# A hybrid decoder layer on one core: value products in wider columns, the solve's row spread in two fp32r passes, and a refitted order

## The chip, the core and the metric

One Trainium2 chip, one of its cores. The time is device microseconds of one execution of the whole kernel, as the median of several runs. The engines are called by their functions: TensorE multiplies matrices (PE in the profile, its weight loads PEld), VectorE (DVE), ScalarE (ACT) and GpSimd (POOL) work elementwise, and SyncE (SP) issues most transfers.

## The reference

One decoder layer on x of 512 tokens by 1024 channels, all in float32:

```
h = x @ w_in                                   # one combined projection
y_a = nsa_attention(...) @ w_nsa_out           # 8 heads, compressed + selected + sliding window, gated
y_b = gated_deltanet(...) @ w_gdn_out          # 4 heads, chunked, a triangular solve in each chunk
mix = (sigmoid(gate_a) * y_a + sigmoid(gate_b) * y_b) @ w_o
x = layer_norm(ALPHA * x + mix)
f = conv_ffn(x)                                # up, causal conv of width 3, silu gate, down
x = layer_norm(ALPHA * x + f)
```

In the attention, the selected and the window branch of a head each come to a causal softmax over 512 keys with a distance penalty, times values of 64 columns. With 8 blocks of 64 keys and the best 8 chosen, the selected branch sees all keys. In the DeltaNet part, each head has, for every chunk of 64 tokens, a unit lower triangular matrix `eye + m` whose inverse T is needed.

## The kernel before, in words

Float32 accuracy is kept by splitting an operand into a rounded high part and the remainder, both in the format fp32r, and multiplying in three passes: high by high, high by low, low by high. A plain fp32 product is also possible, and is used for small ones. Weights stream from memory in tiles; `split_w` (the lines L241 to L252) loads one, rounds the two halves to `wh` and subtracts to get `wl`. Which engine rounds and which subtracts is looked up in the table ENGINE under "wh" and "ws" with the tile's number.

The first stage, to about 345 us, holds both mixers. The work of the two is cut into named steps: i, j, v (key, query and value convolutions of a DeltaNet head), m, n, w (its matrix, the diagonal solve, the inverse), o, y (recurrence and gate), k, q, p, c (attention keys, queries, compressed branch), a and b (the first and the last three score units of an attention head), and g (merge gates). ORDER writes down their order, SHIFT moves each by a number of priority units, and a list scheduler orders each engine's instructions by the resulting priorities. ENGINE assigns single operations to VectorE, ScalarE or GpSimd. Projections for later steps run on TensorE between the small products of the mixers; their results lie in one of two accumulators of the name `gps`, until the convolution (`conv_silu`, L405 to L423) has read all its taps from it. A tap on VectorE reads the accumulator itself; for a tap on GpSimd, ScalarE reads it and GpSimd adds.

Value products. For each attention head there are six units of scores (`scores`), each of 128 queries, of one branch or of both. `flip` transposes the probabilities of one unit, and writes them as high and low (`pth`, L843, and `ptl`, L844) into slots of 128 columns, of which each branch has eight. The units come in the order: queries 256 to 383 and 384 to 511 of the first branch, the same of the second, then 0 to 127 and 128 to 255 of both together. After each second unit, the products with the values (L856) run over two slots at a time, 256 columns, into the accumulator `pout`; slot 6 holds zeros, for the key block that lies beyond the queries of its unit.

The solve. `gdn_tri` inverts the 16x16 diagonal blocks of a head. `lo` is the strictly lower part of m with its sign, `f16` its rows within blocks (L521), and the rows are spread over the partitions by a product with the constant `same` (L529), of a masked copy `gx` (L527), once for 512 columns and once for 256. Fifteen rounds of a multiply and an add on VectorE follow (L536, L537), then `z`. Tiles `lo`, `gx`, `m` and others share the three buffers of the tag "mid"; `m` lives on until the inverse has been built.

After the first stage come the output products of the mixers (lines L262 to L265 with `pm`, L1021 to L1023), the up-projection with its convolution (`pu`, L1100 to L1119), and the down-projection by a seven-product scheme of half matrices (L1147). For it GpSimd issues eight transfers of 2816 KB that add weight blocks in memory (`sums`, L281), during the up-projection.

Of the kernel before, what the change touches and what calls it, by code (L numbers as in the profile page):

```python
# [21 lines left out]
TT = 4  # L22
# [112 lines left out]
def body(ctx: ExitStack, tc: tile.TileContext, d, out):  # L135
    nc = tc.nc
    V, A, G, PE = nc.vector, nc.scalar, nc.gpsimd, nc.tensor

    def E(name, h, d="V"):

        return {"V": V, "G": G, "A": A}[ENGINE.get(f"{name}{h}", d)]

    def bc(ap, shape):
        return ap.to_broadcast(shape)
# [41 lines left out]
    nsa = Rows(ph1, "nsa", 1, side="right")  # L186
    sp = Rows(ph1, "slots", 1, side="right")
    def slot(tag, name, shape=(128, 512), dt=F32):
        return sp.tile(list(shape), dt, name=name, tag=tag, bufs=BUFS[tag])
# [324 lines left out]
    def gdn_tri(h):  # L514
        st = HS[h]
        m = st["m"]

        lo = slot("mid", "lo", c4)
        E("lo", h).tensor_tensor(lo, m, bc(C["low"][:, None, :], c4), op=OP.mult)
        f16 = sp.tile([128, TT, 16], F32, name="f16", bufs=2)  # L520
        V.tensor_reduce(f16, lo.rearrange("p c (b j) -> p c j b", b=8), axis=AX.X, op=OP.add)  # L521
        lx = slot("lx", "lx", (128, TT, 16, 16))
        for r0, n in ((8, 16), (0, 8)):
            rs = slice(r0, r0 + 8)
            sh = (128, TT, 8, n)
            gx = slot("mid", "gx", sh)
            E(f"gx{n}", h).tensor_tensor(gx, bc(f16[:, :, None, :n], sh), bc(C["row"][:, None, rs, None], sh), op=OP.mult)  # L527
            pl = dps(sh)
            PE.matmul(pl, C["same"], gx, start=True, stop=True)  # L529
            A.activation(lx[:, :, rs, :n], pl, AF.Copy)  # L530
        xs = sp.tile([128, TT, 16], F32, name="xs", bufs=2)
        E("xs", h).tensor_copy(xs, bc(C["row"][:, None, :], (128, TT, 16)))
        tmp = sp.tile([128, TT, 16], F32, name="tmp", bufs=2)
        for r in range(15):
            n = 15 - r
            V.tensor_tensor(tmp[:, :, :n], lx[:, :, r + 1:, r], bc(xs[:, :, r:r + 1], (128, TT, n)), op=OP.mult)  # L536
            V.tensor_tensor(xs[:, :, r + 1:], xs[:, :, r + 1:], tmp[:, :, :n], op=OP.add)  # L537
# [288 lines left out]
    def flip(h, u, s):  # L826
# [16 lines left out]
        A.activation(th, pt, AF.Copy)  # L843
        V.tensor_tensor(tl, pt, th.bitcast(F32), op=OP.subtract)  # L844
        if t % 2 == 0:
            return
        if u == 1:
            POUT[h] = po.tile([128, S], F32, name="pout")
        pout = POUT[h]
        for br, _ in parts:  # L850
            for k in range(4 if t > 1 else 2):
                o = pout[:, 256:] if t > 1 else pout[:, :256]
                b = 2 * k if t > 1 else 4 + 2 * k
                w = vcat[:, k, br, g].rearrange("p a b -> p (a b)")
                for i, src in enumerate((pth, ptl)):
                    PE.matmul(o, w, src[:, br, b:b + 2, :], start=(u == 1 and k == 0 and i == 0), stop=False)  # L856
# [409 lines left out]
```

## Time and profile before

| what | value |
|---|---|
| three runs | 851.35, 852.24 and 846.26 us, median 851.35 |
| profiled execution, its own time | 847.99 us |
| its span in the profile | 846.2 us |
| TensorE busy | 826.3 us, 98% |
| VectorE, ScalarE, GpSimd busy | 597.3, 403.0, 164.3 us |
| products of L856 | 192 |
| mean granted clock of TensorE | 0.992 |

Busy time is the share of the span in which an engine had at least one instruction under way. Matmuls overlap: one of 512 columns is shown with about 0.39 us while the next starts 0.23 us after it, so distances between starts give the cost. In rows of groups, the numbers behind the bar are the sum of busy time, the mean of one in ns, and the idle time of the engine before them with what ended it. In a timeline a row has its start, its length, the engine, the line and what is written from what.

### The profile page before, as it was taken

The numbers are of one execution on the slowest core, as the hardware profiler recorded it, in microseconds if no ns is written. First come the engines' busy times: TensorE is split into PE (matmuls) and PEld (weight loads), VectorE is DVE, ScalarE is ACT, GpSimd is POOL, SyncE is SP. The second block draws the span as 40 slices with busy tenths as digits, with TensorE's granted clock in tenths as the row PEclk, the third lists the DMA queues.
The fourth block names the chain that finished last, engine by engine and source line by source line (L and its number), as shares of the span: only waits on it lengthen the run. The fifth ranks groups of instructions, "written<-read, shape, count | busy, mean of one in ns | idle before, by whom it ended". The sixth has DMA issues, their size and how long they took to land.

```text
span 846.2 us, 11884 instructions
## 1 busy us (share of the span) xinstructions
PE 826.3 (98%) x4226; PEld 681.4 (81%) x4226; DVE 597.3 (71%) x1276; ACT 403.0 (48%) x890; POOL 164.3 (19%) x160
## 2 busy tenths in 40 slices
PE   9899899999999999999999999999999999999996
PEld 8777688777778778888888898888888888887874
DVE  5855579986867866674457637777777777768786
ACT  4464377575456777532234113444444444556531
POOL 0354442233136111102200003111112111100000
PEclk9999899999999999999999999999999999999998
DMA  7223111002101110254346007998975922575662
GB/s 273 95 83 100 54 48 51 26 26 75 45 32 66 35 51 26 88 178 134 125 137 237 25 2 269 266 244 253 205 223 153 225 88 77 161 247 176 198 213 100
DMA packets 35051, 108.05 MB, mean 128 GB/s; under 512 B 3248, under 2 KB 4400, under 8 KB 34608
## 3 DMA queue, kind: packets, MB, share of 16 engines
q1 hardware_dynamic: 27696, 84.23, 30.6%
q0 software_dynamic: 7296, 23.07, 11.5%
q8 instruction: 33, 0.54, 0.3%
q14 instruction: 26, 0.21, 0.1%
HBM read 105.19 MB, written 25.17 MB: 154 GB/s over the span
## 4 chain that ended last, share of the span: by engine, by line
PE 84%; DVE 10%; DMA 2%; issue 2%; ACT 1%; SPq 0%; POOL 0%; DVEq 0%; ACTq 0%; POOLq 0%
PE pu L262 9%; PE pu L264 9%; PE pu L265 9%; PE gps L262 7%; PE gps L264 7%; PE gps L265 7%; PE px L1147 5%; PE pz L1147 3%; PE pout L856 2%; PE aps L839 2%; PE pw L1022 2%; PE pw L1023 2%; PE pw L1021 2%; PE pm L265 2%; PE pm L262 2%; PE pm L264 2%
## 5 line engine op out<-in xcount | busy, mean ns | idle before, releaser
L252 DVE TENSOR_TENSOR wl<-raw,wh 128x512 fp32r<-128x512 f32 x140 | 114.1, 816 | 66.9 <-ACT wh L248 62.5
L248 ACT ACTIVATE wh<-raw 128x512 fp32r<-128x512 f32 x136 | 85.5, 631 | 151.4 <-PE pu L264 103.8
L262 PE MATMUL pu<-mh,wh 128*128 128x512 f32 (+1 forms) x384 | 142.7, 372 | 0.0
L264 PE MATMUL pu<-ml,wh 128*128 128x512 f32 (+1 forms) x384 | 142.6, 371 | 0.0
L265 PE MATMUL pu<-mh,wl 128*128 128x512 f32 (+1 forms) x384 | 142.6, 371 | 0.0
L262 PE MATMUL gps<-xh,wh 128*128 128x512 f32 x320 | 129.3, 405 | 3.6 <-DVE xs L537 2.2
L264 PE MATMUL gps<-xl,wh 128*128 128x512 f32 x320 | 129.1, 404 | 0.0
L265 PE MATMUL gps<-xh,wl 128*128 128x512 f32 x320 | 126.8, 398 | 0.0
L265 PEld LDWEIGHTS pu<-mh,wl 128*128 128x128 f32 x384 | 72.3, 188 | 12.6
L262 PEld LDWEIGHTS pu<-mh,wh 128*128 128x128 f32 x384 | 72.3, 188 | 12.4
L264 PEld LDWEIGHTS pu<-ml,wh 128*128 128x128 f32 x384 | 72.3, 188 | 12.4
L262 PEld LDWEIGHTS gps<-xh,wh 128*128 128x128 f32 x320 | 60.4, 189 | 16.6 <-issue 2.9
L1103 DVE SCALAR_TENSOR_TENSOR fa<-pu,fcw,fa 128x511 f32<-128x511 f32 x88 | 65.7, 746 | 10.7 <-ACT fa L1100 9.2
L265 PEld LDWEIGHTS gps<-xh,wl 128*128 128x128 f32 x320 | 60.6, 189 | 10.8 <-issue 0.2
L264 PEld LDWEIGHTS gps<-xl,wh 128*128 128x128 f32 x320 | 60.6, 189 | 10.2 <-issue 0.2
L1109 POOL TENSOR_TENSOR fth<-fth,fa 128x512 f32<-128x512 f32 x22 | 28.6, 1302 | 201.8 <-DVE fa L1103 201.8
L252 POOL TENSOR_TENSOR wl<-raw,wh 128x512 fp32r<-128x512 f32 x36 | 46.3, 1288 | 83.0 <-ACT wh L248 68.8
L1080 ACT ACTIVATE wh<-raw 128x512 fp32r<-128x512 f32 x67 | 40.5, 627 | 39.8 <-DMA raw<-wsum 11.1
L1081 DVE TENSOR_TENSOR wl<-raw,wh 128x512 fp32r<-128x512 f32 x67 | 43.8, 685 | 19.4 <-ACT wh L1080 19.2
L812 ACT ACTIVATE sc<-sc,mn 128x384 f32<-128x384 f32 (+2 forms) x64 | 35.8, 560 | 12.9 <-DVE mn L810 10.7
L295 POOL TENSOR_TENSOR rs<-rs,minus_half 128x1 f32<-128x1 f32 x8 | 7.6, 945 | 166.5 <-DVE rs L980 166.5
L1100 ACT ACTIVATE fa<-pu,fcw 128x512 f32<-128x512 f32 x44 | 29.6, 672 | 10.2 <-PE pu L265 10.2
(330 smaller groups left out, 1689.5 us busy)
## 6 DMA issues: line engine op xcount, KB each, us to landing
raw<-in_up SPq DMA_DIRECT2D x44, 512.0 KB, 4.8
raw<-in_wT SPq DMA_DIRECT2D x40, 512.0 KB, 3.5
wsum<-in_down POOLq DMA_DIRECT2D x6, 2816.0 KB, 24.5
raw<-wsum SPq DMA_DIRECT2D x20, 512.0 KB, 4.2
raw<-in_down SPq DMA_DIRECT2D x15, 512.0 KB, 4.4
wsum<-wsum POOLq DMA_DIRECT2D x2, 2816.0 KB, 12.3
raw<-in_wm SPq DMA_DIRECT2D x8, 512.0 KB, 3.6
raw<-in_wo SPq DMA_DIRECT2D x8, 512.0 KB, 3.6
```

The lines of the kernel that those rows point to most:

```text
L248: A.activation(wh, r, AF.Copy)
L252: eng.tensor_tensor(wl, r, wh.bitcast(F32), op=OP.subtract)
L262: i = PE.matmul(ps, wh[k], mh_(k), start=(k == 0), stop=False)
L264: PE.matmul(ps, wh[k], ml_(k), start=False, stop=False)
L265: PE.matmul(ps, wl[k], mh_(k), start=False, stop=(k == n - 1))
L812: A.activation(s[:, i, :n], s[:, i, :n], AF.Exp, scale=-1.0, bias=mn[:, 0, i:i + 1], accum_out=mn[:, 1, i:i + 1])
L1080: A.activation(hi, raw[:, i], AF.Copy)
L1081: V.tensor_tensor(lo, raw[:, i], hi.bitcast(F32), op=OP.subtract)
L1100: A.activation(acc, ps, AF.Copy, scale=w[:, 2:3])
L1103: V.scalar_tensor_tensor(acc[:, n:], ps[:, :S - n], w[:, i:i + 1], acc[:, n:], op0=OP.mult, op1=OP.add)
L1109: G.tensor_tensor(th, th, g[1], op=OP.mult)
L1147: m = PE.matmul(ps, a[x][:, j, ts], w[y], start=first and i == 0, stop=last and i == 2, skip_group_check=True)
```

## The change

Value products: the buffers for the probabilities get 13 slots a branch in place of 8, slot t + 3k for query block t and key block k. The units come in the order of the queries, the two short ones first. The products of a branch run when its last unit is there: key block 0 over all 512 query columns, block 1 over 384, blocks 2 and 3 over 256 each, with a zero slot for key block 3 of the third query block.

The solve: the constant `same` is copied to fp32r once, on GpSimd. `f16` gets three parts, of which the third is the sum as before, the first its rounding and the second the remainder. Each half of the row spread becomes two fp32r products into the same accumulator, of a masked copy of the high part and of one of the low.

Priorities: ORDER, SHIFT and ENGINE are replaced as a whole. The new ENGINE names an engine for nearly every choice, where many stood at a default before. Among others, it moves the last tap of head 1's query convolution ("cq10") from VectorE to GpSimd, `z`, `gx` and `gy` of head 0 in part to GpSimd, and a number of "ws" and "wh" between engines.

The space in on-chip memory that is set aside for the descriptors of GpSimd's transfers is set to 4096 bytes a partition.

```diff
-SHIFT = {'q0': -193, 'a0': -2348, ...
+SHIFT = {'q0': -145, 'a0': -3160, ...
-ENGINE = {'p16': 'A', 'p55': 'V', ...
+ENGINE = {'p36': 'V', 'p15': 'V', ...
-ORDER = "q0 k0 i0 q1 j0 m0 c n0 w0 i1 j1 v0 v1 p0 o0 a0 y0 b0 a1 b1 m1 a2 b2 n1 w1 i2 j2 o1 y1 m2 v2 a3 n2 q2 w2 b3 o2 y2 q3 g0 p1 k1 i3 j3 a4 b4 m3 a5 n3 w3 g1 g2 b5 v3 o3 a6 g3 b6 a7 g4 b7 g5 y3".split()
+ORDER = "q0 k0 i0 q1 j0 c m0 n0 w0 i1 j1 v0 p0 v1 o0 a0 y0 b0 a1 m1 b1 a2 n1 w1 b2 i2 j2 o1 y1 m2 n2 a3 v2 w2 q2 o2 q3 y2 g0 b3 k1 p1 i3 j3 m3 g1 a4 n3 b4 a5 g2 v3 w3 g3 b5 a6 b6 g4 a7 o3 b7 y3 g5".split()
...
+    same_r = nsa.tile([128, 128], F32R, name="same_r")
...
         V.tensor_copy(upper_r, C["upper"])
+        G.tensor_copy(same_r, C["same"])
...
-        f16 = sp.tile([128, TT, 16], F32, name="f16", bufs=2)
-        V.tensor_reduce(f16, lo.rearrange("p c (b j) -> p c j b", b=8), axis=AX.X, op=OP.add)
+        f16 = sp.tile([128, 3, TT, 16], F32, name="f16", bufs=2)
+        V.tensor_reduce(f16[:, 2], lo.rearrange("p c (b j) -> p c j b", b=8), axis=AX.X, op=OP.add)
+        V.tensor_copy(f16[:, 0].bitcast(F32R), f16[:, 2])
+        V.tensor_tensor(f16[:, 1], f16[:, 2], f16[:, 0], op=OP.subtract)
         lx = slot("lx", "lx", (128, TT, 16, 16))
         for r0, n in ((8, 16), (0, 8)):
             rs = slice(r0, r0 + 8)
             sh = (128, TT, 8, n)
-            gx = slot("mid", "gx", sh)
-            E(f"gx{n}", h).tensor_tensor(gx, bc(f16[:, :, None, :n], sh), bc(C["row"][:, None, rs, None], sh), op=OP.mult)
             pl = dps(sh)
-            PE.matmul(pl, C["same"], gx, start=True, stop=True)
+            for i, e in enumerate(("gx", "gy")):
+                gx = slot("mid", "gx", sh, F32R)
+                E(f"{e}{n}", h).tensor_tensor(gx, bc(f16[:, i, :, None, :n], sh), bc(C["row"][:, None, rs, None], sh),
+                                              op=OP.mult)
+                PE.matmul(pl, same_r, gx, start=(i == 0), stop=(i == 1))
             A.activation(lx[:, :, rs, :n], pl, AF.Copy)
...
-    pth = nsa.tile([128, 2, 8, 128], F32R, name="pth")
-    ptl = nsa.tile([128, 2, 8, 128], F32R, name="ptl")
+    pth = nsa.tile([128, 2, 13, 128], F32R, name="pth")
+    ptl = nsa.tile([128, 2, 13, 128], F32R, name="ptl")
     for t in (pth, ptl):
-        G.memset(t[:, :, 6, :].bitcast(F32), 0.0)
-    UNITS = [((0, 2),), ((0, 3),), ((1, 2),), ((1, 3),), ((0, 0), (1, 0)), ((0, 1), (1, 1))]
+        G.memset(t[:, :, 11, :].bitcast(F32), 0.0)
+    UNITS = [((0, 0), (1, 0)), ((0, 1), (1, 1)), ((0, 2),), ((0, 3),), ((1, 2),), ((1, 3),)]
...
-        first = t - 2 if t > 1 else 4 + t
-        own = (slice(br, br + len(parts)), slice(first, first + 2 * t + 1, 2))
+        own = (slice(br, br + len(parts)), slice(t, 4 * t + 1, 3))
...
-        if t % 2 == 0:
+        if t < 3:
             return
-        if u == 1:
+        if br == 0:
             POUT[h] = po.tile([128, S], F32, name="pout")
         pout = POUT[h]
-        for br, _ in parts:
-            for k in range(4 if t > 1 else 2):
-                o = pout[:, 256:] if t > 1 else pout[:, :256]
-                b = 2 * k if t > 1 else 4 + 2 * k
-                w = vcat[:, k, br, g].rearrange("p a b -> p (a b)")
-                for i, src in enumerate((pth, ptl)):
-                    PE.matmul(o, w, src[:, br, b:b + 2, :], start=(u == 1 and k == 0 and i == 0), stop=False)
-        if u < 5:
+        for k in range(4):
+            c = min(k, 2)
+            w = vcat[:, k, br, g].rearrange("p a b -> p (a b)")
+            for i, src in enumerate((pth, ptl)):
+                PE.matmul(pout[:, 128 * c:], w, src[:, br, 3 * k + c:3 * k + 4, :],
+                          start=(br == 0 and k == 0 and i == 0), stop=False)
+        if br == 0:
             return
...
-    nc = bacc.Bacc("TRN2", target_bir_lowering=False, num_devices=1)
+    nc = bacc.Bacc("TRN2", target_bir_lowering=False, num_devices=1, dynamic_dma_scratch_size=4096)
```

More of the change, by code (lines that the diff above doesn't have):

```diff
@@ L126 @@
 LATE = 2500
-SHIFT = {'q0': -193, 'a0': -2348, 'b0': -2285, 'a1': -2210, 'b1': -330, 'a2': -197, 'q3': -550, 'j3': -1663, 'a4': -1622, 'g2': 1524, 'o2': -2902, 'i1': -138, 'b5': -2781, 'y2': 147, 'q1': -7406, 'g1': -1529, 'y3': 6625, 'y1': 53, 'b3': -761, 'k0': -68, 'm2': -702, 'g3': 637, 'b6': 362, 'v2': 240, 'j1': -112, 'm0': -5504, 'b7': -5643, 'o3': 1155, 'y0': 203, 'q2': 4142, 'g4': -1463, 'm3': -2997, 'v0': -140, 'j0': -2134, 'v1': 41, 'o1': -4704, 'v3': 274, 'o0': -1428, 'n2': -847, 'g0': -122, 'b2': -55, 'k1': -1459, 'j2': 105, 'p0': 215, 'a3': 46, 'm1': -1324, 'n3': 240, 'n1': -1535, 'i0': -1541, 'a5': -49, 'p1': -115, 'i2': -71, 'i3': 77, 'n0': -13, 'a6': 272, 'g5': 1119, 'b4': -10, 'a7': 1035, 'w2': -801, 'w3': 118, 'w1': -1404, 'w0': 29, 'c': 6}
@@ L128 @@
-ENGINE = {'p16': 'A', 'p55': 'V', 'p24': 'A', 'p32': 'A', 'vb0': 'A', 'p43': 'A', 'p04': 'G', 'p54': 'A', 'p20': 'G', 'kd2': 'A', 'p25': 'A', 'kd0': 'V', 'p06': 'A', 'vb1': 'A', 'lo3': 'G', 'p44': 'A', 'p45': 'V', 'p34': 'G', 'p36': 'A', 'kd1': 'A', 'kd3': 'A', 'sq1': 'V', 'xs3': 'G', 'vb2': 'A', 'wh31': 'V', 'ws4': 'V', 'ws11': 'V', 'ws29': 'G', 'p03': 'V', 'wh2': 'A', 'wh43': 'G', 'p37': 'A', 'ws43': 'V', 'wh42': 'G', 'ws30': 'G', 'wh8': 'V', 'ws14': 'G', 'wh32': 'G', 'wh35': 'G', 'ws15': 'G', 'sq3': 'V', 'y1': 'V', 'z3': 'V', 'wh0': 'V', 'wh36': 'A', 'wh38': 'G', 'wh1': 'A', 'ws1': 'V', 'ws18': 'V', 'ws38': 'V', 'p26': 'V', 'wh39': 'G', 'sv2': 'V', 'sk0': 'G', 'p33': 'V', 'ws16': 'G', 'ws36': 'G', 'ws40': 'V', 'ws5': 'G', 'p47': 'V', 'xs2': 'G', 'ck2': 'V', 'wh34': 'A', 'ws21': 'G', 'wh46': 'G', 'ws42': 'V', 'wh47': 'G', 'ws32': 'V', 'wh44': 'V', 'ws34': 'V', 'ws39': 'V', 'lo0': 'G', 'gx80': 'V', 'gx81': 'G', 'gx82': 'G', 'gx83': 'V', 'xs1': 'G', 'ws27': 'G', 'sv0': 'G', 'ws0': 'V', 'wh5': 'A', 'wh22': 'A', 'ws9': 'V', 'wh6': 'A', 'wh17': 'A', 'cv1': 'V', 'wh37': 'G', 'ws25': 'V', 'ws17': 'V', 'ws20': 'V', 'wh14': 'V', 'wh30': 'A', 'cv2': 'G', 'wh33': 'V', 'ws28': 'V', 'cv21': 'G', 'ws35': 'G', 'wh24': 'V', 'ck0': 'G', 'y2': 'A', 'p46': 'A', 'ck1': 'G', 'ck30': 'V', 'p07': 'A', 'p56': 'A', 'y3': 'V', 'z2': 'G', 'ws13': 'G', 'ws12': 'V', 'ws31': 'V', 'p57': 'A', 'gx160': 'V', 'wh13': 'G', 'p17': 'G', 'wh4': 'A', 'ws19': 'V', 'sk3': 'G', 'wh21': 'G', 'wh28': 'A', 'wh15': 'A', 'ws37': 'V', 'p22': 'A', 'ws33': 'V', 'wh16': 'G', 'ws24': 'V', 'ck31': 'V', 'vb3': 'V', 'xs0': 'G', 'wh3': 'A', 'ws10': 'V', 'wh12': 'A', 'ws23': 'G', 'p05': 'A', 'wh11': 'V', 'ws26': 'V', 'wh25': 'V', 'wh26': 'V', 'cq32': 'V', 'p23': 'A', 'cv11': 'G', 'wh23': 'A', 'p53': 'G', 'wh10': 'A', 'wh18': 'V', 'wh7': 'G', 'wh20': 'V', 'cq31': 'V'}
@@ L129 @@
-ORDER = "q0 k0 i0 q1 j0 m0 c n0 w0 i1 j1 v0 v1 p0 o0 a0 y0 b0 a1 b1 m1 a2 b2 n1 w1 i2 j2 o1 y1 m2 v2 a3 n2 q2 w2 b3 o2 y2 q3 g0 p1 k1 i3 j3 a4 b4 m3 a5 n3 w3 g1 g2 b5 v3 o3 a6 g3 b6 a7 g4 b7 g5 y3".split()
+SHIFT = {'q0': -145, 'a0': -3160, 'b0': -2897, 'a1': -1567, 'b1': -1214, 'a2': -669, 'q3': -440, 'j3': -2154, 'a4': -1760, 'g2': 2211, 'o2': -4563, 'i1': -138, 'b5': -1422, 'y2': 402, 'q1': -8014, 'g1': -1551, 'y3': 8737, 'y1': 59, 'b3': -1705, 'k0': 2, 'm2': -8060, 'g3': 1693, 'b6': 0, 'v2': -39, 'j1': -105, 'm0': -4343, 'b7': -399, 'o3': 198, 'y0': 69, 'q2': 1367, 'g4': -13060, 'm3': -869, 'v0': 51, 'j0': -3953, 'v1': 20, 'o1': -5670, 'v3': 718, 'o0': -2311, 'n2': -8069, 'g0': -2749, 'b2': 104, 'k1': -1999, 'j2': 125, 'p0': 153, 'a3': -126, 'm1': -2337, 'n3': -71, 'n1': -1122, 'i0': -1387, 'a5': -724, 'p1': -116, 'i2': -116, 'i3': 286, 'n0': -13, 'a6': -114, 'g5': 541, 'b4': 688, 'a7': 1553, 'w2': 6, 'w3': 139, 'w1': -1280, 'w0': 197, 'c': -18}
@@ new lines @@
+ENGINE = {'p36': 'V', 'p15': 'V', 'p44': 'A', 'p52': 'A', 'vb0': 'A', 'p03': 'A', 'p24': 'G', 'p14': 'A', 'p40': 'V', 'kd2': 'A', 'p45': 'A', 'kd0': 'V', 'p26': 'V', 'vb1': 'A', 'lo3': 'G', 'p04': 'A', 'p05': 'V', 'p54': 'G', 'p56': 'A', 'kd1': 'A', 'kd3': 'A', 'sq1': 'V', 'xs3': 'G', 'vb2': 'A', 'wh31': 'V', 'ws4': 'V', 'ws11': 'V', 'ws29': 'V', 'p23': 'V', 'wh2': 'A', 'wh43': 'V', 'p57': 'A', 'ws43': 'V', 'wh42': 'V', 'ws30': 'V', 'wh8': 'V', 'ws14': 'G', 'wh32': 'G', 'wh35': 'G', 'ws15': 'V', 'sq3': 'V', 'y1': 'V', 'z3': 'V', 'wh0': 'A', 'wh36': 'G', 'wh38': 'G', 'wh1': 'G', 'ws1': 'V', 'ws18': 'V', 'ws38': 'G', 'p46': 'V', 'wh39': 'V', 'sv2': 'V', 'sk0': 'G', 'p53': 'V', 'ws16': 'V', 'ws36': 'V', 'ws40': 'V', 'ws5': 'V', 'p07': 'A', 'xs2': 'G', 'ck2': 'V', 'wh34': 'G', 'ws21': 'G', 'wh46': 'G', 'ws42': 'V', 'wh47': 'G', 'ws32': 'G', 'wh44': 'A', 'ws34': 'G', 'ws39': 'V', 'lo0': 'G', 'gx80': 'V', 'gx81': 'G', 'gx82': 'G', 'gx83': 'V', 'xs1': 'V', 'ws27': 'G', 'sv0': 'G', 'ws0': 'V', 'wh5': 'V', 'wh22': 'G', 'ws9': 'V', 'wh6': 'A', 'wh17': 'A', 'cv1': 'V', 'wh37': 'V', 'ws25': 'G', 'ws17': 'V', 'ws20': 'V', 'wh14': 'V', 'wh30': 'A', 'cv2': 'G', 'wh33': 'G', 'ws28': 'V', 'cv21': 'V', 'ws35': 'V', 'wh24': 'V', 'ck0': 'G', 'y2': 'A', 'p06': 'A', 'ck1': 'G', 'ck30': 'G', 'p27': 'A', 'p16': 'A', 'y3': 'G', 'z2': 'G', 'ws13': 'G', 'ws12': 'V', 'ws31': 'V', 'p17': 'A', 'gx160': 'G', 'wh13': 'G', 'p37': 'G', 'wh4': 'V', 'ws19': 'V', 'sk3': 'G', 'wh21': 'G', 'wh28': 'A', 'wh15': 'A', 'ws37': 'G', 'p42': 'A', 'ws33': 'G', 'wh16': 'A', 'ws24': 'V', 'ck31': 'V', 'vb3': 'V', 'xs0': 'V', 'wh3': 'A', 'ws10': 'V', 'wh12': 'A', 'ws23': 'V', 'p25': 'A', 'wh11': 'V', 'ws26': 'V', 'wh25': 'A', 'wh26': 'V', 'cq32': 'V', 'p43': 'A', 'cv11': 'V', 'wh23': 'A', 'p13': 'G', 'wh10': 'A', 'wh18': 'V', 'wh7': 'A', 'wh20': 'V', 'cq31': 'V', 'cq22': 'G', 'p10': 'A', 'p35': 'A', 'p12': 'A', 'p11': 'V', 'wh19': 'V', 'p41': 'G', 'lo2': 'V', 'cv12': 'V', 'ck10': 'V', 'cq0': 'V', 'p20': 'A', 'wh9': 'A', 'p00': 'V', 'ck32': 'V', 'p34': 'V', 'ws45': 'G', 'sk2': 'V', 'ws8': 'V', 'cv31': 'V', 'ck20': 'V', 'ck12': 'V', 'sq0': 'V', 'ws46': 'V', 'p51': 'A', 'cv10': 'V', 'wh41': 'V', 'p47': 'G', 'ws3': 'G', 'cq30': 'V', 'p50': 'V', 'gx163': 'V', 'p21': 'G', 'ck21': 'V', 'gx161': 'V', 'wh40': 'A', 'z1': 'V', 'cv20': 'V', 'sv1': 'V', 'gy161': 'V', 'lo1': 'G', 'cq21': 'G', 'gy162': 'V', 'ws22': 'G', 'gy160': 'G', 'ws41': 'V', 'ws7': 'G', 'gy82': 'V', 'cv22': 'V', 'wh45': 'V', 'sk1': 'V', 'cq10': 'G', 'ws6': 'G', 'p32': 'V', 'p30': 'V', 'wh29': 'V', 'gy80': 'G', 'z0': 'G', 'sq2': 'V', 'wh27': 'G', 'ws47': 'G', 'sv3': 'V', 'cv0': 'G', 'p01': 'V', 'cv32': 'V', 'cq11': 'V', 'cq1': 'V', 'gy83': 'V', 'p22': 'V', 'gy81': 'V', 'p33': 'V', 'ws2': 'G', 'ck22': 'V', 'cq20': 'V', 'y0': 'V', 'ws44': 'V'}
```

## The prediction

> **What bounds the kernel now.** I read the page first: the engines' busy time, the clock row, the chain that ended last.
>
> ```profile
> span 846.2 us, 11884 instructions
> PE 826.3 (98%) x4226; PEld 681.4 (81%) x4226; DVE 597.3 (71%) x1276; ACT 403.0 (48%) x890; POOL 164.3 (19%) x160
> PEclk9999899999999999999999999999999999999998
> PE 84%; DVE 10%; DMA 2%; issue 2%; ACT 1%; SPq 0%; POOL 0%; DVEq 0%; ACTq 0%; POOLq 0%
> ```
>
> TensorE is busy for 98% of the span and carries 84% of the chain, so work taken from TensorE is time. Only 19.9 us (846.2 - 826.3) are idle there. The table by stage (length, then busy time of PE, PEld, DVE, ACT, POOL, granted clock, DMA) says where:
>
> ```profile
> 0.00:345.00 345.00, 334.83 (x1959) 272.78 (x1960) 247.99 (x751) 201.63 (x563) 106.42 (x108) 0.99 0.21 67
> 500.00:735.00 235.00, 235.00 (x1088) 196.74 (x1087) 172.17 (x256) 100.31 (x172) 38.58 (x30) 1.00 0.70 191
> 735.00:847.00 112.00, 101.54 (x442) 81.93 (x440) 83.89 (x133) 52.47 (x83) 3.82 (x4) 0.97 0.56 185
> ```
>
> Everything that the change touches (both mixers) lies in the first 345 us: 10.2 us of idle TensorE there, and VectorE at 72% (248.0 of 345). The up-projection after 500 us has no idle TensorE, and the 10.5 us idle in the last stage belong to its own output, which the change leaves alone. So the sum has two parts: TensorE time removed, and what the new order does to those 10.2 us. The largest piece of them is at 90 us, in the solve of head 0:
>
> ```profile
> 90.00:92.60 2.60, 0.39 (x3) 0.04 (x1) 2.53 (x9) 0.07 (x1) 0.00 (x0) 1.00 0.66 202
> 92.60:99.60 7.00, 6.94 (x26) 6.06 (x27) 2.28 (x5) 2.83 (x5) 3.18 (x3) 0.51 0.00 1
> 90.13 0.74 DVE L413 SCALAR_TENSOR_TENSOR acc<-gps,tiny,acc 128x511 f32<-128x511 f32 x1
> ...
> 91.69 0.75 DVE L413 SCALAR_TENSOR_TENSOR acc<-gps,tiny,acc 128x509 f32<-128x509 f32 x1
> 92.36 0.16 DVE L537 TENSOR_TENSOR xs<-xs,tmp 128x4 f32<-128x4 f32 x1
> ...
> 92.59 0.65 PE L262 MATMUL gps<-xh,wh 128*128 128x512 f32 x1 [2.21 <-DVE xs L537]
> ```
>
> TensorE stands still for 2.21 us until VectorE, busy without a break with solve steps (L537) and convolution taps (L413), has read a projection out of its accumulator. Then the clock is at 0.51 for 7.0 us, which loses 7.0 x 0.49 = 3.4 us. This stall costs 2.2 + 3.4 = 5.6 us. A shorter one kept the full clock:
>
> ```profile
> 40.16 0.47 PE L262 MATMUL gps<-xh,wh 128*128 128x512 f32 x1 [1.18 <-ACT tap L410]
> 36.00:41.00 5.00, 2.69 (x15) 1.97 (x14) 3.12 (x11) 2.36 (x6) 3.43 (x4) 1.00 0.03 7
> ```
>
> The Trainium skill, "TensorE: Matmul & The Clock Gate", section on the HAM clock gate, says that the clock halves after an idle window of about 3.4 us of a free-running counter. By that rule a stall of 2.21 us should usually cost itself alone; the rows show the half clock after it, so the row decides here, and the page's free-running window allows the loss to differ between executions.
>
> **Part 1, value products.** Busy times of matmuls overlap, so I price them by distances between starts.
>
> ```profile
> L856 PE MATMUL pout<-pth,vcat 128*128 128x256 f32 x96 | 26.4, 299 | 0.0
> L856 PE MATMUL pout<-ptl,vcat 128*128 128x256 f32 x96 | 24.8, 290 | 0.0
> 135.47 0.28 PE L856 MATMUL pout<-ptl,vcat 128*128 128x256 f32 x1
> 135.59 0.39 PE L861 MATMUL pout<-pch,vm 128*128 128x512 f32 x1
> 135.82 0.40 PE L861 MATMUL pout<-pcl,vm 128*128 128x512 f32 x1
> ...
> 136.57 0.33 PE L807 MATMUL aps<-kl,q 128*128 128x384 f32 x1
> 136.74 0.38 PE L628 MATMUL dps<-vn,at 128*128 128x128 f32 x2
> ```
>
> 256 columns take 0.12 us, 384 take 0.17, 512 take 0.23 (the start of the next row less the own). Before: 192 of these products over 8 heads, 24 a head, 24 x 0.12 = 2.88 us. After: for each branch and each of hi and lo, key blocks of 512, 384, 256 and 256 columns, so 16 a head: 4 x 0.23 + 4 x 0.17 + 8 x 0.12 = 2.56 us. Removed: 0.32 x 8 = **2.6 us**. Transposes, evictions and scores are the same in number and size. The thirteen slots take the place of eight, and the order of units puts the diagonal blocks first: the products now come in two batches of eight (after the fourth and sixth unit) instead of three.
>
> ```profile
>   ACT pth L843: 4.4, 2
> ```
>
> That row, of who waited for the products, is the cost today of a slot that is rewritten right after it was read: 4.4 us of ScalarE in two waits. After, the first unit of the next head rewrites the slot 0 that the last batch has just read, while the fifth and sixth units no longer do so inside a head. Behind a waiting ScalarE eviction stand the exponentials of the next score and the rounded weights. ScalarE is busy for 58% of the stage (201.6 of 345), and that room hides it: 0 us; without cover, one batch of 1.3 us for each of 7 head changes, 9 us at worst, and 4 us gained at best if all of today's waits went.
>
> **Part 2, the solve's row spread.** Per head one product of 512 columns and one of 256, in plain fp32:
>
> ```profile
> L529 PE MATMUL dps<-gx,cst 128*128 128x512 f32 x8 | 4.3, 614 | 0.5 <-DVE gx L527 0.5
> 157.51 0.28 PE L856 MATMUL pout<-pth,vcat 128*128 128x256 f32 x1
> 157.64 1.46 PE L529 MATMUL dps<-gx,cst 128*128 128x512 f32 x4
> 158.74 0.47 PE L856 MATMUL pout<-ptl,vcat 128*128 128x256 f32 x1
> 159.05 0.28 PE L856 MATMUL pout<-pth,vcat 128*128 128x256 f32 x1
> L491 PE MATMUL dps<-grh,upper_r 128*128 128x512 f32 x4 | 1.9, 484 | 0.0
> ```
>
> Eight records for four products: each is two passes. From 157.64 to 159.05 are 1.41 us for both, less 0.12 for the product at 158.74: 1.29 us a head. After: two passes of 0.23 and two of 0.12, 0.70 us; that such an fp32r product of another prepared tile (L491, 484 ns long, against 614) behaves like its neighbours is the row for it. Removed: 0.59 x 4 = **2.4 us**, up to 3.2 where L529 stood between fp32r products, since the 158.74 row took 0.31 instead of 0.12. Added per head: a rounding and a subtraction of 64 columns, and a second masked multiply for each half.
>
> ```profile
> L527 DVE TENSOR_TENSOR gx<-f,cst x6: 410/685/1067, 67.7 to 276.6; 128x512 f32<-128x512 f32 x4, 128x256 f32<-128x256 f32 x2
> L537 DVE TENSOR_TENSOR xs<-xs,tmp x60: 126/194/1144, 80.3 to 303.6; 128x60 f32<-128x60 f32 x4, 128x56 f32<-128x56 f32 x4, 128x52 f32<-128x52 f32 x4, 128x48 f32<-128x48 f32 x4
> L252 DVE TENSOR_TENSOR wl<-raw,wh 128x512 fp32r<-128x512 f32 x31 | 22.6, 732 | 3.4 <-ACT wh L248 2.5 <-PE gps L265 0.2
> L252 POOL TENSOR_TENSOR wl<-raw,wh 128x512 fp32r<-128x512 f32 x32 | 41.1, 1288 | 74.6 <-ACT wh L248 60.5 <-ACT pth L843 4.8 <-PE dps L427 3.9
> ```
>
> Two small ones of about 0.2 us (by L537) and about 0.69 + 0.41 for the multiplies: 1.5 us a head, 6 us of VectorE in all, less what the tables give to GpSimd. Against TensorE this is nothing where projections stand between, as in 76 to 78 us. There is a new wait, though: the tiles of tag "mid" have three buffers, one holds m, so the third and fourth multiply (gx8, gy8) wait until TensorE has read the first and second. Behind a waiting multiply stand the taps that free the projections' accumulators. Its bounds: below, 0; above, one stall like that at 90 us, 5.6 us, per head. I take 0, since TensorE waited for this step only once (0.5 us).
>
> **Part 3, the tables.** Of the weight tiles, lows of 12 go from GpSimd to VectorE and of 6 back, and VectorE gets the rounded highs of 6 more than it gives away, two halves each: 12 x 0.73 = 9 us for the lows by L252, 12 x 0.45 = 5 us for the highs by the row below, while 6 scalings and 3 taps that leave VectorE on balance return some 5.
>
> ```profile
> L250 DVE CAST wh<-raw 128x512 fp32r<-128x512 f32 x19 | 8.5, 453 | 6.8 <-PE gps L264 6.8
> ```
>
> With part 2 VectorE goes from 248 to about 263 us, 76%: it remains below TensorE. In favour: the last tap of head 1's query convolution, the row at 91.69, moves to GpSimd; ScalarE then reads the accumulator in its place, and TensorE's 2.21 us would be 0.75 shorter. Since the whole order of the stage is new, I put the refit at 0, with the stall's 5.6 us to win as one end and the same to lose as the other.
>
> The smaller scratch for GpSimd's transfers could make an issue wait for the ones before it:
>
> ```profile
> 510.58 1.25 POOL L281 DMA_DIRECT2D wsum<-in_down  x1
> 527.78 1.77 POOL L281 DMA_DIRECT2D wsum<-in_down  x1
> 537.23 1.29 POOL L1109 TENSOR_TENSOR fth<-fth,fa 128x512 f32<-128x512 f32 x1 [7.68 <-DVE fa L1103]
> wsum<-in_down POOLq DMA_DIRECT2D x6, 2816.0 KB, 24.5
> ```
>
> If the third waited until the first had landed, GpSimd would stand from 527.8 to 535.1 (510.6 + 24.5), and its next work is at 537.2: 7.68 us of idle time hide it, 0 us. The copy of "same" sits on GpSimd where it waits for the constants already: 0.
>
> **Sum.** 2.6 + 2.4 = 5.0 us off. The profiled execution took 847.99 us (span 846.2 and 1.8 around it), so 843.0 on its scale. It lies 3.4 under the median of the three runs; all four average 849.5, and from that I forecast **844.5 us**.
>
> **Rivals.**
> A: the refit also removes the stall at 90 us. For it: the tap at 91.69 leaves VectorE, and 1.46 us would be left, near the 1.18 that kept the clock. Against: the solve of head 0 gets longer by its own added steps. 844.5 - 5.6 = 838.9. By the window alone that the Trainium skill states on that page, the stall would be worth its own length, 844.5 - 2.2 = 842.3.
> B: one new stall of that kind, 850.1.
> C, the other side: gx8 or gy8, waiting for TensorE, holds VectorE or GpSimd in the solve; the accumulators come free over 2 us late and the clock halves, in three heads or four. 849.5 - 5.0 + 3 x 5.6 = 861.3; from three it is over 1% slower. For it: head 3 has all four multiplies on VectorE, and VectorE was 97% busy in the stall (2.53 of 2.60). Against: in three of four heads today nothing of the sort happened.
> D: the fp32r passes do not save (they wait for each other's tiles, or the passes take 0.35 us each): 844.5 + 2.4 = 846.9.
>
> **Numbers.** Forecast 0.48, A 0.31, B 0.11, C 0.05, D 0.05. About 1% (8.5 us) is what a measurement of this kernel can tell from no change. Faster by over 1% means under 842.8: A, and a tail of the forecast, 0.36; slower, over 859.9: C and a tail of B, 0.08; the rest 0.56. The range goes from A with a further 2.3 us (TensorE's idle time from 36 to 41 us, 5.00 - 2.69) to two new stalls, 844.5 + 11.2: 836 to 855.
>
> **What would show it.** L856 with 128 records, 32 each of 512 and 384 columns, 64 of 256, and 16 records of 512 or 256 columns for the spread with a length near 390 and 285 ns; TensorE's matmul count down by 64; idle TensorE before 345 us near 10 us; the first projection of the later stages starting 5 us earlier. For A the clock row has no drop near 90 us; for C it has more drops, each after a wait for VectorE or GpSimd in the solve. I am wrong if the idle time of the first stage changes by more than the 5.0 us taken away.

## The result and the profile after

The changed kernel takes 854.33 us (median of ten runs, 852.95 to 855.64) against 848.57 of the kernel before in the same measurement (843.65 to 852.32). The ratio is 1.0064, with a 95% interval of 1.004 to 1.0089: 0.6% slower, where 0.5 to 0.6% faster was forecast. The profiled execution took 853.89 us. Three lines of its page:

```profile
span 852.1 us, 11742 instructions
PE 821.4 (96%) x4162; PEld 673.5 (79%) x4162; DVE 610.9 (72%) x1295; ACT 401.5 (47%) x890; POOL 171.8 (20%) x168
PEclk9999999999999999999999999999999999999998
```

TensorE has 64 matmuls fewer (4226 to 4162) and is busy 4.9 us less (826.3 to 821.4). The span is 5.9 us longer all the same, so TensorE's idle time rose from 19.9 to 30.7 us (852.1 - 821.4). The work went away; the gaps between the work grew by twice as much.

The table by stretch tells where. Its columns: the stretch, its length, busy time of PE, PEld, DVE, ACT and POOL with instructions, the granted clock, the share and the rate of DMA. First before, then after:

```profile
0.00:100.00 100.00, 93.34 (x451) 77.47 (x452) 62.63 (x160) 44.47 (x109) 34.37 (x40) 0.97 0.38 127
100.00:200.00 100.00, 97.94 (x637) 78.73 (x636) 82.92 (x265) 70.00 (x214) 33.20 (x33) 1.00 0.12 38
200.00:300.00 100.00, 98.60 (x573) 79.22 (x573) 77.72 (x235) 58.01 (x160) 29.43 (x27) 1.00 0.15 48
0.00:355.10 355.10, 344.91 (x2005) 280.83 (x2006) 256.60 (x765) 208.41 (x576) 106.42 (x108) 0.99 0.21 68
```

```profile
0.00:100.00 100.00, 90.09 (x445) 74.07 (x446) 65.54 (x166) 45.10 (x109) 34.10 (x41) 0.98 0.39 127
100.00:200.00 100.00, 94.28 (x599) 74.17 (x597) 82.71 (x263) 70.18 (x216) 33.21 (x33) 1.00 0.12 37
200.00:300.00 100.00, 95.70 (x543) 75.53 (x542) 80.45 (x234) 56.39 (x162) 32.99 (x31) 1.00 0.15 49
0.00:359.50 359.50, 339.56 (x1941) 272.97 (x1942) 270.64 (x788) 210.20 (x580) 104.21 (x108) 1.00 0.21 67
500.00:735.00 235.00, 235.00 (x1106) 197.48 (x1105) 171.74 (x253) 98.80 (x169) 37.91 (x29) 1.00 0.68 187
```

The fourth row of each ends where the first `pm` product starts, the end of the first stage: 355.1 us before and 359.5 after. Up to there TensorE is busy 5.4 us less (344.9 to 339.6) and idle 9.7 us more (355.1 - 344.9 = 10.2; 359.5 - 339.6 = 19.9): 4.4 us later. In each of the three stretches of 100 us TensorE is busy for about as much less, 3.3, 3.7 and 2.9 us. No single stall explains it: ahead of `pm`, waits of under 1 us sum to 4.2 us before and 11.4 after, the longer ones to 6.0 and 8.5. After that the two kernels run alike to the first down-projection product (730.1 and 734.5 us), with TensorE full in the up-projection, and the last stage adds the remaining 1.5 us.

Who made TensorE wait ahead of `pm` (engine, line, what it waited for; us in total, times, longest), first before, then after; smaller rows and those that hardly changed are left out. The new code is some lines longer: L839, L823 and L529 of before are L845, L829 and L535 of after.

```profile
PE gps L262 <- DVE xs L537: 2.2, 1, 2.2
PE aps L839 <- ACT sc L821: 0.5, 1, 0.5
PE dps L529 <- DVE gx L527: 0.5, 1, 0.5
PE aps L839 <- POOL sc L823: 0.4, 1, 0.4
```

```profile
PE dps L429 <- POOL z L545: 4.2, 2, 3.8
PE aps L845 <- DVE sc L829: 4.2, 5, 2.0
PE gps L262 <- ACT qf L696: 1.2, 2, 1.0
PE dps L535 <- POOL gx L533: 1.2, 3, 0.6
PE aps L845 <- POOL sc L829: 1.1, 3, 0.6
PE dps L535 <- DVE gx L533: 0.9, 1, 0.9
```

The stall at head 0's solve is still there, longer and of another kind: TensorE waited 2.21 us for an accumulator, and now waits 3.85 us for `z`, the result of the solve itself. The clock halves behind it as it did before, for a shorter time (below). The largest increase is new: score transposes (L845) wait 5.3 us for the scaling of the scores (L829), 0.4 before.

```profile
95.84 0.66 PE L429 MATMUL dps<-ident,z 128*128 128x128 f32 x4 [3.85 <-POOL z L545]
96.00:100.00 4.00, 4.00 (x18) 3.52 (x18) 1.08 (x2) 1.28 (x2) 2.42 (x4) 0.58 0.00 0
```

### The profile page after: what moved, and what is told of

The parts are those of the page before. It is cut to its first block, busy times and chain, and to the rows that moved or that the text cites. A ratio compares the mean times of both kernels' runs of the same rounds, so it can differ in the third digit from the quotient of the medians.

```text
span 852.1 us, 11742 instructions
## 1 busy us (share of the span) xinstructions
PE 821.4 (96%) x4162; PEld 673.5 (79%) x4162; DVE 610.9 (72%) x1295; ACT 401.5 (47%) x890; POOL 171.8 (20%) x168
## 3 DMA queue, kind: packets, MB, share of 16 engines
q0 software_dynamic: 7296, 23.07, 11.4%
## 4 chain that ended last, share of the span: by engine, by line
PE 56%; DVE 7%; DMA 3%; issue 1%; ACT 1%; POOL 0%; DVEq 0%; ACTq 0%
PE pu L265 9%; PE pu L264 9%; PE pu L262 9%; PE gps L265 3%; PE gps L262 3%; PE gps L264 3%; PE px L1151 3%; DMA raw<-wsum 2%; DVE wl L1085 2%; PE pu L1151 2%; PE pw L1026 2%; PE pw L1025 2%; PE pm L264 2%; PE pm L262 2%; PE pw L1027 2%; PE pm L265 2%
## 5 line engine op out<-in xcount | busy, mean ns | idle before, releaser
L252 DVE TENSOR_TENSOR wl<-raw,wh 128x512 fp32r<-128x512 f32 x146 | 120.6, 830 | 61.7 <-ACT wh L248 56.3
L248 ACT ACTIVATE wh<-raw 128x512 fp32r<-128x512 f32 x126 | 79.4, 631 | 127.9 <-PE pu L264 96.4
L265 PE MATMUL gps<-xh,wl 128*128 128x512 f32 x320 | 128.8, 405 | 0.0
L1113 POOL TENSOR_TENSOR fth<-fth,fa 128x512 f32<-128x512 f32 x22 | 31.0, 1410 | 167.1 <-DVE fa L1107 167.1
L1084 ACT ACTIVATE wh<-raw 128x512 fp32r<-128x512 f32 x67 | 39.9, 626 | 42.1 <-DMA raw<-wsum 16.3
L1085 DVE TENSOR_TENSOR wl<-raw,wh 128x512 fp32r<-128x512 f32 x67 | 43.5, 683 | 21.3 <-ACT wh L1084 21.2
L252 POOL TENSOR_TENSOR wl<-raw,wh 128x512 fp32r<-128x512 f32 x30 | 39.1, 1304 | 38.2 <-ACT wh L248 25.9
L845 PE MATMUL aps<-ident,sc 128*128 128x128 f32 x160 | 28.9, 279 | 6.5 <-DVE sc L829 4.2
```

The costliest lines, as they stand in the source:

```text
L248: A.activation(wh, r, AF.Copy)
L252: eng.tensor_tensor(wl, r, wh.bitcast(F32), op=OP.subtract)
L265: PE.matmul(ps, wl[k], mh_(k), start=False, stop=(k == n - 1))
L1084: A.activation(hi, raw[:, i], AF.Copy)
L1085: V.tensor_tensor(lo, raw[:, i], hi.bitcast(F32), op=OP.subtract)
L1113: G.tensor_tensor(th, th, g[1], op=OP.mult)
```

## The experiments

Theory F: the gain of the edits is real, but ORDER, SHIFT and ENGINE are fitted to one exact set of instructions, and any edit draws a new order of the whole stage; what the time does depends on the fit of that order. Its rival is S: single costs of the edits (the solve's added VectorE steps and waits, the later score batches, the scratch) make up the loss. A later rival, L: operations moved to GpSimd hold up VectorE, and moving them back repairs it. For F the last runs have a rival R, that the changed tables are a middling draw with many as good. The first four runs went by an earlier pair, T (the new tables make the loss) and W (the new code's own waits make it).

All runs are in one table: the median, the ratio to the kernel before in the same measurement with its 95% interval, and from the profile the start of the first `pm` product and TensorE's idle time ahead of it. The kernel before had medians of 848.6 to 851.8 us in the four measurements, so losses are given against it in the same measurement.

| kernel | median us | ratio | first pm us | idle us |
|---|---|---|---|---|
| before | 848.57 | 1 | 355.1 | 10.2 |
| after | 854.33 | 1.0064 [1.004, 1.0089] | 359.5 | 19.9 |
| e1_new_code_old_tables | 872.49 | 1.0253 [1.0219, 1.0287] | 377.0 | 26.7 |
| e2_old_code_new_tables | 881.73 | 1.0351 [1.032, 1.0383] | 383.4 | 31.7 |
| e3_products_old_tables | 881.59 | 1.0343 [1.0318, 1.0368] | 385.5 | 32.1 |
| e4_solve_old_tables | 879.73 | 1.0332 [1.0305, 1.0358] | 384.5 | 31.9 |
| n1_ticks | 885.18 | 1.0404 [1.0373, 1.0435] | 391.7 | 31.0 |
| n2_scratch | 851.16 | 0.9993 [0.9971, 1.0016] | 352.0 | 10.5 |
| f1_solve0 | 855.83 | 1.0055 [1.0028, 1.0083] | 360.0 | 19.5 |
| f2_all_unlocked | 861.21 | 1.0125 [1.0099, 1.0151] | 367.8 | 23.6 |
| a1_one_tick | 883.77 | 1.0393 [1.0365, 1.0422] | 391.1 | 38.7 |
| a6_ticks | 861.93 | 1.0136 [1.0114, 1.0158] | 367.1 | 24.4 |

**Code and tables apart.** The changed code with the old ORDER, SHIFT and ENGINE, and the old code with the new ones; the score units, whose numbers the change renames, keep the engines that they had.

```diff
 e1: -SHIFT, ENGINE, ORDER of after    +SHIFT, ENGINE, ORDER of before   (code of after)
 e2: -SHIFT, ENGINE, ORDER of before   +SHIFT, ENGINE, ORDER of after    (code of before)
```

> All edits of the changed kernel, with ORDER, SHIFT and ENGINE of before (the units of scores keep their old engines under their new numbers; gy stays on VectorE). Theory T (the new tables make the loss): TensorE's 5.0 us are saved and the first stage's idle time stays near 10 us, so 848.6 - 5.0 = 843.6 us. Rival W (the new code's own waits make it: the multiplies that wait for a buffer of the tag mid, the slots that are rewritten right after the last batch): the loss stays, 853 to 856 us, with over 17 us of idle TensorE before 345 us.

> The code of before with the new ORDER, SHIFT and ENGINE (units of scores mapped back to their old numbers). Theory T: the tables cost 10.8 us (the added idle time of TensorE, 30.7 less 19.9) whatever the code is: 848.6 + 10.8 = 859.4 us. Rival W: the tables alone cost nothing, 848.6 us. If the tables fit only their own code, something above 848.6 comes out too, so the first run has to decide together with this one.

Both crosses lose over 20 us, the one with the lighter work too, and neither T nor W forecast that. So the refit is no small item with a zero beside it: without it the changed code costs 20.7 us against before (872.5 - 851.8), with it 5.8 (854.3 - 848.6), so it is worth some 15 us.

**One edit alone, old tables.** e3 has the value products in wider columns only, e4 the solve's row spread only, both with the smaller scratch.

```diff
 e3: gdn_tri of before, UNITS and flip of after
 e4: gdn_tri and same_r of after, UNITS and flip of before
```

> The value products in 512, 384 and 256 columns alone, with the old solve and the old tables, and the smaller scratch that the buffers need. Theory T: 848.6 - 2.6 = 846.0 us. Rival W, if it is the slots rewritten right after the last batch or the two large batches: 852 us or more, with ScalarE's evictions pth waiting for the products.

> The row spread in two fp32r passes alone, with the old products and the old tables, and the smaller scratch. Theory T: 848.6 - 2.4 = 846.2 us. Rival W, if it is gx8 and gy8 waiting for a buffer: 852 us or more, with TensorE idle before the second pair of spread products in several heads, and the clock halved there.

Each alone costs 28 to 30 us, where T and W had 846 and 852 us or more, and both together (e1) cost only 21. Costs of single edits add up; these do not. In both, the largest loss is no wait of the edited lines. The waits of TensorE, first e3, then e4:

```profile
PE gps L262 <- ACT qf L690: 6.6, 2, 6.3
PE aps L839 <- ACT sc L821: 2.5, 2, 2.1
```

```profile
PE gps L262 <- ACT qf L696: 6.4, 2, 6.2
PE gps L262 <- DVE mn L820: 3.2, 1, 3.2
```

Projections wait over 6 us for an accumulator that ScalarE reads (`qf`, an attention query, which no part of the change touches); the table by stretch of e3 shows the clock at 0.86 there, where it is 1.00 in both the kernel before and the changed one:

```profile
200.00:250.00 50.00, 40.77 (x224) 30.45 (x222) 25.35 (x71) 16.20 (x43) 10.47 (x9) 0.86 0.10 32
```

**No edit at all.** The kernel before, with six priority units added after each of the four solve steps, as many as the changed solve has more instructions. No instruction is added, removed or changed. n2 is the kernel before with the smaller scratch alone.

```diff
 n1:
-            at += tc.tile_snap_priority() - p0
+            at += tc.tile_snap_priority() - p0 + (6 if step[0] == "n" else 0)
 n2:
-    nc = bacc.Bacc("TRN2", target_bir_lowering=False, num_devices=1)
+    nc = bacc.Bacc("TRN2", target_bir_lowering=False, num_devices=1, dynamic_dma_scratch_size=4096)
```

> The code and the tables of before, with no instruction added or removed; only the running count from which every later step's priority is taken goes up by 6 after each of the four solve steps, as much as the solve's edit adds. About a third of TensorE's order comes out differently. Theory F (a table is fitted to one exact order of the instructions, and any other draw from the same tables is worse): 858 to 875 us, though no engine has more work. Rival S (order is robust, and the runs with the old tables lost by the work and the waits of the new code): 848.6 us within 3.

> Before, with the smaller scratch for the descriptors of GpSimd's transfers alone; the order on TensorE is the same. GpSimd should wait at some issues of the eight large transfers, as in the changed kernel (21.2 us in two waits before issues there), and nothing of it should reach the end: 848.6 us within 2. Rival: the waits delay the product fth of the up-projection and so TensorE, 852 us or more.

n1 takes 885 us, the slowest of all runs and 10 us above what F forecast, with not one instruction changed. Moving a few priorities is enough to lose 34 us, so the losses of e1 to e4 need no cost of their edits to explain them, and they don't support S. TensorE's waits in n1 are of the kind of e3 and e4, and the clock is lower too:

```profile
PE gps L262 <- ACT qf L690: 3.5, 2, 3.2
PE gps L262 <- DVE xs L537: 3.3, 1, 3.3
200.00:250.00 50.00, 42.40 (x233) 31.96 (x232) 26.22 (x80) 19.91 (x62) 12.24 (x12) 0.88 0.11 32
0.00:391.70 391.70, 360.69 (x2004) 289.92 (x2005) 264.00 (x765) 209.76 (x575) 106.36 (x108) 0.95 0.19 61
```

The last row is n1's whole first stage. It ends 36.6 us later than before (391.7 - 355.1): 20.8 us of that are idle time (31.0 - 10.2), and 15.8 us are the same products taking longer (360.7 - 344.9), nearly all of it at half clock. A wait can thus be paid twice, as idle time and as half clock after it. In this execution 3.9 of the 36.6 us were lost ahead of 70 us, where no engine's order differs from before yet, so they are not the shift's.

The scratch costs nothing (0.9993, the interval holds 1), as predicted.

**Repairs of the changed kernel.** f1 puts head 0's `z` and one weight subtraction from GpSimd on VectorE; f2 moves the masked `lo` of heads 1 and 3 as well, which stand beside the stretched scalings of the last section.

```diff
 f1: ENGINE z0: 'V', ws2: 'V'
 f2: ENGINE z0: 'V', ws2: 'V', lo1: 'V', lo3: 'V'
```

> The changed kernel with two entries of ENGINE set back to VectorE: z of head 0 and the low part of weight tile 2; the orders stay as they are but for these. Theory L (GpSimd's operations that read on-chip memory stop VectorE's solve steps, which TensorE waits for at 92 to 96 us): one of the stretched steps goes (1.1 us) and z gets 0.4 us shorter, against 1.4 us of added work on VectorE: 853 to 854 us, the stall of 3.85 us about 1 us shorter. Rival R (the moves to GpSimd were a gain): 855 to 857 us.

> As the run before, and the masked copies lo of heads 1 and 3 set back to VectorE as well, so that the scalings of scores at 145 and 277 us, which were stretched to 2.70 and 2.49 us, meet one GpSimd operation in place of two. Theory L: TensorE's 1.99 us at 148 and 1.05 us at 278 shrink by about half each, in all 851 to 852.5 us. Rival R: the waits turn up elsewhere, 854 us or more.

f1 is as slow as the changed kernel (1.0055 and 1.0064 to before, intervals over each other), and f2 is slower; both came out as their rival R had them. L falls as a repair. In f1 the stall did not shrink, it is 4.2 us long. `z` itself is shorter on VectorE (0.69 us) than it was on GpSimd (1.05), and follows at once on the last step of the solve, but that step ends 2.3 us later. The first row below is of the changed kernel, the others are of f1:

```profile
94.49 0.17 DVE L543 TENSOR_TENSOR xs<-xs,tmp 128x4 f32<-128x4 f32 x1
96.78 0.17 DVE L543 TENSOR_TENSOR xs<-xs,tmp 128x4 f32<-128x4 f32 x1
96.98 0.69 DVE L545 TENSOR_TENSOR z<-xs,cst 128x512 f32<-128x512 f32 x1
PE dps L429 <- DVE z L545: 4.2, 1, 4.2
```

VectorE does the weight subtraction (0.69 us) ahead of the solve's steps now, and as many of these steps are stretched as before, other ones. TensorE's order is left as it was in f1: 3 of its 1941 products ahead of `pm` stand elsewhere. So f1 tries L without a new order.

In f2 TensorE waits less for the scalings on VectorE, 1.9 us against 4.2, but the new order ends the first stage 8 us later, with idle time of other kinds (23.6 us in all):

```profile
PE aps L845 <- ACT sc L827: 2.1, 3, 0.8
PE aps L845 <- DVE sc L829: 1.9, 4, 0.8
PE aps L845 <- DVE tmp L542: 1.1, 1, 1.1
```

**The changed kernel, with its priorities shifted.** One unit (a1) and six units (a6) after each solve step, as in n1.

```diff
-            at += tc.tile_snap_priority() - p0
+            at += tc.tile_snap_priority() - p0 + (1 if step[0] == "n" else 0)     # a6: 6
```

> The changed kernel, with one priority unit added after each solve step (n0 to n3), so that everything behind them in ORDER is later by one to four units; no instruction is added, removed or changed. Theory F (the tables are fitted to one exact order, the changed kernel's as much as the one before): the redrawn order loses 10 to 30 us against the changed kernel, 865 to 885 us, with the idle time of TensorE before the first pm product up from 19.9 to 30 us or more. Rival R (the changed tables were a middling draw, so that a neighbour is as good): 850 to 858 us, idle 15 to 24 us.

> The same with six units after each solve step, as in the run of the kernel before with six units, which took 885 us; no instruction is changed. Theory F: 865 to 885 us, idle before the first pm product 30 us or more. Rival R: 850 to 858 us.

a1 loses some 28 us against the changed kernel (33.5 over the kernel before in its measurement, less 5.8), as F said; a6 loses some 6 (11.7 less 5.8), between the two expectations. A single unit costs more than six, so the loss doesn't grow with the size of the shift. Neither neighbour is as good as the changed tables, so R fails in these two tries: as far as they tell, the tables are a fit, not a middling draw. The waits of a1 are of the same kinds again:

```profile
PE dps L429 <- POOL z L545: 5.6, 1, 5.6
PE aps L768 <- ACT qf L696: 4.9, 1, 4.9
PE aps L845 <- ACT sc L827: 4.3, 4, 2.3
PE gps L262 <- ACT tap L412: 2.6, 1, 2.6
```

How far an order moved can be counted in the traces: the products of TensorE ahead of `pm` that lie outside the longest sequence which a run shares with the kernel that it was made from. There are 373 of 2004 in n1, and of 1941 there are 460 in a1, 204 in f2, 186 in a6 and 3 in f1; n2 has none. The losses go with it roughly: 34, 28, 5 and 6 us, and none in f1 and n2. So not every edit draws the order anew, as F had it: f1's did not.

## Why the prediction was wrong

**Part 1, value products: right.** 128 products are there, in the three widths predicted. The groups of the line, and the group of the row spread:

```profile
L859 PE MATMUL pout<-pth,vcat x64: 274/310/577, 133.7 to 339.0; 128*128 128x256 f32 x32, 128*128 128x512 f32 x16, 128*128 128x384 f32 x16
L859 PE MATMUL pout<-ptl,vcat x64: 276/335/500, 134.7 to 339.1; 128*128 128x256 f32 x32, 128*128 128x512 f32 x16, 128*128 128x384 f32 x16
L535 PE MATMUL dps<-gx,same_r x16: 278/388/500, 77.6 to 291.4; 128*128 128x512 f32 x8, 128*128 128x256 f32 x8
```

The distances from each start to the next, less idle time, sum to 23.3 us for the products, against 25.7 before: 2.4 off, where 2.6 was predicted.

**Part 2, the solve's row spread: right where nothing waits, about 1 us short in all.** There are 16 records of two widths. Where nothing waits, the spacing is 0.23 us for 512 columns (those of 77.6, 78.3 and 153.3 us) and 0.12 for 256 (218.9 and 291.4 us), as the sum had it, so rival D is wrong there. With waits for the masked copies the distances are longer, up to 0.48 us without the idle time: the sixteen passes take 3.9 us, where the sum had 4 x 0.70 = 2.8. That much of D's mechanism came. The new wait for the buffers was taken as 0: TensorE waited 2.1 us in four times for `gx` and `gy` (1.2 + 0.9 in the rows of the waits; 0.5 before). Rival C's mechanism exists, at 2.1 us instead of three times 5.6.

Of the 5.4 us less busy time ahead of `pm`, some 1.7 are no work: the clock was halved for 7.0 us before and for some 4 after, 7.0 x 0.49 = 3.4 against 4.0 x 0.42 = 1.7. That leaves 3.7 against the predicted 5.0. n2 bears the correction out: with the order of before and the full clock throughout, TensorE is busy for 341.5 us there, 3.4 less than before. Most of the missing 1.3 us lies in the sixteen passes above; seven of the nine long ones stand beside waits.

**Part 3, the refit at 0, with ends of 5.6 us either way: the step that failed.** The stage's idle time rose by 9.7 us, against the 5.0 taken away, which is the condition that the prediction named for being wrong. So the term put at 0 measured 9.7 us of idle time, beyond its end of 5.6. Its ends were one stall of the order at hand, while n1, with no instruction changed, shows that a new order can cost 34 us. The changed code with the old tables cost 20.7 us; the refit won back some 15 of them, and had to win over 20 to win anything. That the time lies inside the stated 836 to 855 us is luck, from a wide range: the change went the other way. The prediction looked for the stall at 90 us as what a refit might win, and it did not go: the last step of the solve, `z`, moved to GpSimd and was done at 95.8 us, since VectorE reached the end of the solve's rounds at 94.7, where it had been 92.5. Rival A's premise, the tap leaving VectorE, came true and was not enough.

Rival B, one new stall worth 5.6 us, comes nearest in time (850.1), not in mechanism: the loss lies mostly in waits of under 1 us (4.2 to 11.4 us), and the two longest are 3.85 and 1.99 us. By line, the waits for scaled scores grew by 4.9 us, those for `gx` and `gy` by 1.6, and the stall at head 0's solve by 1.6.

**Scratch and copy of `same`:** right at 0. In the changed kernel GpSimd does stand at the issue of the large transfers, and its idle time hides it:

```profile
POOL wsum L281 <- issue: 21.2, 2, 12.2
```

**What stays open** is whether a better fit of the tables to the new code exists. The new work is 5.0 us lighter by its clean distances and 3.7 as measured; no order tried here had less idle time on the changed code than 19.5 us, and the kernel before runs with 10.2. That the change can't be faster is not shown. Nor is it shown how much of the 9.7 us is a poorer fit and how much belongs to the edits: the waits for `gx` and `gy` (1.6 us) are new with the solve's edit, and the order of the score units, which the first edit changes, also decides when the scalings come that TensorE waits for. Neither edit was tried in an unchanged order; with each, the scheduler drew the stage anew.

## What to carry to other kernels

Where a list scheduler's priorities were fitted to the kernel, an edit's own saving is one number and the redrawn order is another, and the second may be several times the first: size it by moving a priority by one unit and changing no instruction, before any edit is judged. The bottleneck engine's idle time, with the half clock behind it, then bounds what a refit can win (10.2 and 3.4 us in this stage), and the spread of the shifted orders says what it can lose (34 us here). A predicted range that takes its ends from one stall of the present order is too narrow.

## What the runs showed of the hardware

A stall of the same length halved the clock in one execution and not in another. n2 has the TensorE work of the kernel before in the same order; its stall at the same place is 2.20 us long (2.21 before), and the clock stays at 1.00, where before it was at 0.51 from 92.6 to 99.6 us:

```profile
92.34 0.47 PE L262 MATMUL gps<-xh,wh 128*128 128x512 f32 x1 [2.20 <-DVE xs L537]
96.00:100.00 4.00, 4.00 (x48) 2.78 (x47) 2.32 (x5) 1.88 (x5) 1.49 (x2) 1.00 0.02 4
```

So the 3.4 us of half clock that the prediction priced into each stall is not due every time; by itself it moves the time between executions (the first `pm` product comes at 352.0 us in n2, at 355.1 before).

The clock records kept in the traces tell the two apart. In each of the twelve traces the clock changes only at points of a grid of 3.41 us, and half clock in the first stage lasts one to four steps of it (6.83 us before, 3.41 after, 13.65 in e3). In the kernel before, the whole stall lies in one step, from 89.3 to 92.7 us; in n2, with the grid reckoned back from the one change at the end of its span, a step ends at 92.0 us and divides the stall into 1.86 and 0.34 us. Of all steps of the twelve first stages that began at full clock, each of the 21 with 1.99 us or more of idle TensorE was followed by half clock; of the eight with 1.67 to 1.86 us five were, and of some 1200 with less only three, which stay unexplained.

This agrees with the free-running window of the Trainium skill, "TensorE: Matmul & The Clock Gate", section on the HAM clock gate, as far as the phase goes; that 2.2 us can suffice at all is not what a window of about 3.4 us leads one to expect.

Some VectorE operations stand for as long as GpSimd works beside them. The scaling of 256 columns takes 0.40 us alone and 2.70 us beside two GpSimd operations, and TensorE waits for it:

```profile
145.24 2.70 DVE L829 TENSOR_SCALAR sc<-sc,mn,gsig 128x256 f32<-128x256 f32 x1
145.31 1.26 POOL L521 TENSOR_TENSOR lo<-m,cst 128x512 f32<-128x512 f32 x1
146.54 1.25 POOL L513 TENSOR_TENSOR at<-at,cst 128x512 f32<-128x512 f32 x1
148.00 0.44 PE L845 MATMUL aps<-ident,sc 128*128 128x128 f32 x2 [1.99 <-DVE sc L829]
148.46 0.40 DVE L829 TENSOR_SCALAR sc<-sc,mn,gsig 128x256 f32<-128x256 f32 x1
```

The scaling's end at 147.9 us lies at the end of the second GpSimd operation (147.8). The same happens to a solve step, which has two inputs of 28 columns:

```profile
90.33 1.28 POOL L413 TENSOR_TENSOR acc<-acc,tap 128x509 f32<-128x509 f32 x1 [0.31 <-ACT tap L412]
90.34 1.31 DVE L543 TENSOR_TENSOR xs<-xs,tmp 128x28 f32<-128x28 f32 x1
92.81 0.19 DVE L543 TENSOR_TENSOR xs<-xs,tmp 128x28 f32<-128x28 f32 x1
```

The last row is of f1, where nothing runs beside the same step. The Trainium skill, "SBUF — State Buffer", section "Who interferes with whom", says that VectorE and GpSimd share a pair of ports, that one of them holds it for a whole instruction and the other stands still, and names operations with two inputs in that memory and scalings in a two-port mode among those concerned; the rows agree. The time by which VectorE operations of the first stage are longer beside GpSimd than the shortest of their kind sums to some 13 us in 19 operations before and 21 us in 27 after. That these 8 us are part of the lost time is argued from the waits of TensorE for scalings on VectorE (L829, 4.2 us in five, none among the rows before), and not shown: f1, which kept TensorE's order, still has some 20 us of it in 28 operations, so it did not take the overlaps away, and f2 redrew the order.
